# A pair's seven products in another order, with three sums formed in PSUM, and W2's gathered sums scaled by token

## The chip, the cores and the metric

The kernel runs on one core of a Trainium2 chip. The metric is the device time of one execution in microseconds (us). Five engines with queues of their own work side by side and wait for each other through semaphores: TensorE (PE, with its weight loads as PEld), VectorE (DVE), ScalarE (ACT), GpSimd (POOL) and SyncE (SP), which here only issues DMAs. Each engine takes its instructions in the order in which they stand in its queue.

## What is computed

Two layers of an encoder over 512 tokens with 1024 channels. Cut to what matters here, a layer is

```
u    = rms_norm(h)
proj = u @ w_in                      # q, k, v of three mixers, and 3 x 1024 gate logits
a, r, c = differential attention, retention, grouped-query attention
merged  = sum_n sigmoid(gate_logits[n]) * (branch[n] @ w_branch[n])
h = h + merged @ w_out
m = relu(rms_norm(h) @ w_mlp_in) ** 2          # 1024 -> 4096
h = h + m @ w_mlp_out                          # 4096 -> 1024
```

All of it is in float32 accuracy. Each matrix product is done as three passes over halves: an operand is split into `hi` (its value in TensorE's shorter float32r) and `lo` (the rest), and hi*hi + hi*lo + lo*hi is summed in PSUM.

## The kernel before

Activations lie channel-major: a tile holds 128 channels by 512 tokens. A *unit* is 128 output channels of a product, 24 matmuls over 512 tokens. Some units are done in *pairs* (the `w1` units, 16 pairs per layer, and 7 pairs of gate units per layer) with a two-by-two scheme that needs seven products instead of eight: the two units' weights form A, A12, A21, A22 and four sums S1 to S4, the tokens are cut in a left half (`lt`) and a right half (`rt`), and product n (1 to 7) is 12 matmuls over 256 tokens. `pair` (L704) runs them, `product` (L697) issues one, `right` (L686) picks its token operand, and DVE and ACT join the products into the tiles `c0` and `c1`. For W2's first three groups a scheme of the same kind works over larger blocks (`wide_product`, L1477): its seven results are added up in DRAM (`sums`) by accumulating DMAs, and `gather` (L1498) reads them back, joins them, turns them with TensorE transposes and adds them to `h`.

The weights of a unit come by one 512 KB DMA into one of two `stage` buffers. For a pair (`cut_pair`, L567) two such loads are cut: ACT casts `w_hi`, DVE subtracts `w_lo`, and DVE forms `sa` and `sb`, which are cast and cut as well. So a pair's weights become ready in the order: those of products 1 and 2 (`stage`), of products 5 and 6 (`sa`), of 3 and 7 (`sb`); those of 4 (a 512-wide `stage`) lie between.

All operations are first recorded. `Plan.order` (L347) then replays the record with a price per operation and sends each engine's queue out in the order of that replay: the operation recorded earliest goes first among those whose inputs are ready and whose buffers are free. An instruction waits on the chip for what it needs, wherever the replay put it. PSUM has pools of banks `mm` (3), `sc` (2), `tr` (2) and `av` (1); a pair takes one bank each of `mm`, `sc` and `tr`. Where a helper records an operation, the profile gives its line as L455 (matmul), L457 (transpose) or L461 (anything else).

In a layer of some 890 us the mixers with their projections come first (to about 410 us in layer 0), then the gate pairs woven with the branches' projections (`x` and `proj`, 410 to 516), the output projection (`wo`, to 560), `w1` pairs woven with W2's wide products (`x` and `wide`, 560 to 850), and W2's last group with the gather (`w` and `turn`, to 900). Layer 1 does the same some 892 us later.

Of the kernel before, what the change touches and what calls it, by code (L numbers as in the profile page):

```python
# [13 lines left out]
AF = mybir.ActivationFunctionType  # L14
ALU = mybir.AluOpType
# [456 lines left out]
class Core:  # L472
# [152 lines left out]
        self.nc.scalar.activation(out=hi, in_=src, func=AF.Copy, scale=r)  # L625
        self.nc.vector.scalar_tensor_tensor(out=lo, in0=src, scalar=r, in1=hi, op0=ALU.mult, op1=ALU.subtract)

    def passes(self, out, terms, start=True, stop=True):
        n = len(terms)
        for i, (x, y) in enumerate(terms):  # L630
            self.nc.tensor.matmul(out=out, lhsT=x, rhs=y, start=start and i == 0, stop=stop and i == n - 1)

    def transpose(self, out, in_):
        self.nc.tensor.transpose(out=out, in_=in_, identity=self.ident)
# [59 lines left out]
            return u["v"][j][p][:, lt if n == 6 else rt]  # L694
        return u["w"][j // 2][p][:, (j % 2) * 256:(j % 2) * 256 + 256]

    def product(self, out, w, u, n):  # L697
        hi, lo = w[n]
        for j in range(4):
            c = slice(j * 128, (j + 1) * 128)  # L700
            xh, xl = self.right(u, n, 0, j), self.right(u, n, 1, j)
            self.passes(out, [(hi[:, c], xh), (hi[:, c], xl), (lo[:, c], xh)], j == 0, j == 3)

    def pair(self, l, key, u, kinds, out):  # L704

        nc = self.nc
        w = self.weights(l, key)
        lt, rt = slice(0, 256), slice(256, 512)
        c0, c1 = self.g("c0"), self.g("c1")
        tmp = self.g("pu")  # L710
        x = self.psum(kinds[0], "x17")
        y = self.psum(kinds[1], "x26")
        z = self.psum(kinds[2], "x45")
        add = lambda out, p, r: nc.vector.tensor_tensor(out=out, in0=p, in1=r, op=ALU.add)
        self.product(x[:, lt], w, u, 1)
        nc.scalar.copy(out=tmp[:, lt], in_=x[:, lt])
        for j, f in enumerate(u.pop("t1", [])):
            for i in range(2):
                o = [u["u"][p][2 * j + i][:, rt] for p in range(2)]
                self.split(f[:, i * 256:(i + 1) * 256], *o)  # L720
        yield
        two = lambda v: v.rearrange("p (a b) -> p a b", a=2)
        wide = lambda v: v.unsqueeze(1).to_broadcast([128, 2, 256])
        self.product(y[:, lt], w, u, 2)
        yield
        self.product(y[:, rt], w, u, 6)
        add(two(c0), two(y), wide(tmp[:, lt]))
        yield
        self.product(z[:, rt], w, u, 5)
        yield  # L730
        self.product(x[:, rt], w, u, 7)
        add(tmp[:, rt], x[:, rt], c0[:, rt])
        add(c0[:, rt], z[:, rt], c0[:, rt])
        yield
        self.product(z[:, lt], w, u, 4)
        add(two(c1), two(z), wide(tmp[:, rt]))
        yield
        self.product(y[:, lt], w, u, 3)
        add(c0[:, rt], y[:, lt], c0[:, rt])
        out += [c0, c1]  # L740

    def add_square(self, x, acc):
# [650 lines left out]
    def mlp(self, l, mT, h, mid, load, ready):  # L1393
        nc = self.nc
        u, acc = {"u": self.new_u(), "v": [], "w": []}, None
        for i in (0, 4, 1, 5, 2, 6, 3, 7):
            p = self.psum("mm", "wo")
            hi, lo = self.weights(l, ("wo", i))
# [4 lines left out]
                self.feed_pair(h, i - 4, 2 * l + 1, u)  # L1403
            acc = self.add_square(h[i], acc)
            nc.sync.dma_start(out=mid[i], in_=h[i])
        _, _, r2 = self.rms(acc, True)
        ms = [[] for _ in range(4)]
        for what, g, i in mlp_order():
            m = ms[g]
# [18 lines left out]
                self.wide_product(l, g, i, now)  # L1428
                continue
            if i == 0:  # L1430
                gather = self.gather(h, mid, load, r2)
            if i in GATHERED:
                next(gather)
            hi, lo = self.weights(l, ("w2", g, i))
# [60 lines left out]
            else:  # L1495
                nc.gpsimd.dma_start(out=self.sums[n, s], in_=y, accum_op=ALU.add)

    def gather(self, h, mid, load, r2):  # L1498

        nc = self.nc  # L1500

        def back(n, s):
            x = self.g("wp")
            nc.sync.dma_start(out=x, in_=self.sums[n, s])
            return x

        tt = lambda out, x, y, op=ALU.add: nc.vector.tensor_tensor(out=out, in0=x, in1=y, op=op)
        u2, c = [None, None], [[None] * 4, [None] * 4]
        for s in range(2):
            p1, p2, p6, p5, p3 = (back(n, s) for n in (1, 2, 6, 5, 3))  # L1510
            tt(p2, p1, p2)
            tt(p6, p6, p1, ALU.subtract)
            tt(p5, p5, p6)
            tt(p3, p3, p5, ALU.subtract)
            c[0][s], c[0][2 + s], u2[s] = p2, p3, (p6, p5)
        for half in range(2):
            if half:
                for s in range(2):
                    p7, p4 = back(7, s), back(4, s)
                    p6, p5 = u2[s]  # L1520
                    tt(p5, p5, p7, ALU.subtract)
                    tt(p6, p6, p7, ALU.subtract)
                    tt(p6, p6, p4)
                    c[1][s], c[1][2 + s] = p6, p5
            for i in range(4):
                k = half * 4 + i
                h[k] = load(mid, k)
                p = self.psum("tr", "turn")
                for t in range(4):
                    self.transpose(p[:, t * 128:(t + 1) * 128], c[half][t][:, i * 128:(i + 1) * 128])  # L1530
                y = self.g("y")
                nc.vector.tensor_tensor(out=y, in0=p, in1=r2, op=ALU.mult)
                nc.vector.tensor_tensor(out=h[k], in0=h[k], in1=y, op=ALU.add)
            yield

    def last_unit(self, hi, lo, m, r2, x, ready):
# [163 lines left out]
```

## Time and profile before

| | |
|---|---|
| device time, 3 runs | 1787.8 us median (1786.89 to 1788.88) |
| the profiled execution | 1790.48 us, its span 1788.7 us, mean granted clock 0.996 |
| PE busy | 1751.3 us, 98% of the span |
| DVE busy | 1521.9 us, 85% |
| ACT busy | 1082.3 us, 61% |
| DMA | 201.94 MB, mean 113 GB/s |

A matmul's record is longer than the distance to the next one, since they are pipelined; the distance from start to start is what one costs on a busy PE. Names in the profile stand without buffer numbers, so the tiles `x17`, `x26` and `x45` of a pair all read `x`; products 1 to 3 and 5 are told by `u` on the right, 6 and 7 by `t23`, 4 by `t4`.

### The profile page before, as it was taken

The page shows a single profiled execution, that of the slowest core. Times are in us where ns is not written, and L with a number is a line of the kernel's source. Part 1 is how long each engine was busy: PE and PEld are TensorE (multiplying, and loading weights), DVE is VectorE, ACT ScalarE, POOL GpSimd, SP SyncE. Part 2 cuts the span into 40 slices and gives each one's busy share as a digit, 9 for nine tenths or more (in the row PEclk, how much of TensorE's full clock was granted, in tenths as well). Part 3 has the DMA queues.
Part 4 walks back from the last instruction along what each step waited for, and adds up shares of the span by engine and source line. Part 5 has one row for each costly group of instructions (what it writes and reads, how often), then busy time and mean ns, then how long its engine had stood idle before and what let it go on. Part 6 is the DMA issues. An engine that isn't in the chain of part 4 may idle for free.

```text
span 1788.7 us, 27147 instructions
## 1 busy us (share of the span) xinstructions
PE 1751.3 (98%) x10136; PEld 1529.1 (85%) x10136; DVE 1521.9 (85%) x2500; ACT 1082.3 (61%) x1864; POOL 345.5 (19%) x350
## 2 busy tenths in 40 slices
PE   8999999999999999998999999999999999999999
PEld 6887888889989999887887778888898899998887
DVE  8866797899979999898967677978999799999986
ACT  5545676784446767666445456767844467667650
POOL 2334472002210001111012334710012100011110
PEclk9999999999999999999999999999999999999999
DMA  6311212212345254746542112121133452646482
GB/s 203 106 59 55 88 55 71 60 36 95 112 166 171 95 201 99 196 95 180 192 137 68 59 62 80 49 71 59 36 95 129 149 171 99 209 99 184 95 242 88
DMA packets 76740, 201.94 MB, mean 113 GB/s; under 512 B 8896, under 2 KB 9408, under 8 KB 76608
## 3 DMA queue, kind: packets, MB, share of 16 engines
q1 hardware_dynamic: 68544, 185.53, 31.6%
q0 software_dynamic: 8064, 14.68, 5.5%
q8 instruction: 79, 1.29, 0.3%
q14 instruction: 53, 0.43, 0.1%
HBM read 169.77 MB, written 30.41 MB: 112 GB/s over the span
## 4 chain that ended last, share of the span: by engine, by line
PE 68%; DVE 15%; DMA 5%; ACT 4%; issue 4%; POOL 3%; SPq 0%; DVEq 0%; ACTq 0%; POOLq 0%
PE x L455 17%; PE wide L455 6%; PE gate L455 6%; PE proj L455 5%; PE w L455 5%; PE wo L455 5%; DVE w_lo L461 4%; DMA stage<-in_w 4%; PE c L455 4%; DVE c L461 3%; PE wtr L457 2%; PE rg L455 2%; PE gsc L455 2%; PE gav L455 2%; DVE sb L461 2%
## 5 line engine op out<-in xcount | busy, mean ns | idle before, releaser
L461 ACT CAST w_hi<-stage 128x1024 fp32r<-128x1024 f32 (+1 forms) x235 | 226.5, 968 | 214.1 <-DMA stage<-in_w 127.6
L461 DVE TENSOR_TENSOR w_lo<-stage,w_hi 128x1024 fp32r<-128x1024 f32 (+1 forms) x235 | 279.4, 1191 | 18.6 <-ACT w_hi L461 14.9
L455 PE MATMUL x<-u,w_hi 128*128 128x256 f32 x1472 | 278.8, 287 | 4.9 <-DVE c L461 4.9
L455 PEld LDWEIGHTS x<-u,w_hi 128*128 128x128 f32 x1472 | 236.5, 195 | 11.2 <-DVE c L461 7.9
L455 PE MATMUL x<-u,w_lo 128*128 128x256 f32 x736 | 210.1, 288 | 8.8 <-DVE w_lo L461 8.8
L461 POOL DMA_DIRECT2D sums<-wp x56 | 49.1, 907 | 566.8 <-ACT wp L461 558.7
L455 PEld LDWEIGHTS x<-u,w_lo 128*128 128x128 f32 x736 | 143.1, 195 | 9.9 <-DVE w_lo L461 9.7
L455 PE MATMUL wide<-w_hi,xh 128*128 128x512 f32 x336 | 129.4, 391 | 2.7 <-ACT wp L461 2.7
L455 PE MATMUL wide<-w_lo,xh 128*128 128x512 f32 x336 | 131.2, 390 | 0.0
L455 PE MATMUL wide<-w_hi,xl 128*128 128x512 f32 x336 | 130.7, 390 | 0.0
L461 ACT ACTIVATE c<-c 128x512 f32<-128x512 f32 x156 | 98.5, 632 | 51.8 <-DVE c L461 49.1
L461 DVE TENSOR_TENSOR w_lo<-A,w_hi 128x512 fp32r<-128x512 f32 x168 | 112.2, 683 | 11.3 <-ACT w_hi L461 11.2
L461 ACT CAST w_hi<-A 128x512 fp32r<-128x512 f32 x168 | 100.7, 619 | 19.2 <-DVE A L461 9.5
L455 PE MATMUL gate<-u,w_hi 128*128 128x512 f32 x320 | 106.4, 399 | 0.0
L455 PE MATMUL x<-t23h,w_lo 128*128 128x256 f32 x368 | 104.6, 284 | 0.2
L455 PE MATMUL x<-t23h,w_hi 128*128 128x256 f32 x368 | 104.3, 284 | 0.0
L455 PE MATMUL x<-t23l,w_hi 128*128 128x256 f32 x368 | 104.1, 283 | 0.0
L455 PE MATMUL c<-w_hi,u 128*128 128x512 f32 x256 | 86.1, 394 | 0.0
L461 ACT CAST w_hi<-sa 128x1024 fp32r<-128x1024 f32 x46 | 48.5, 1053 | 62.0 <-DVE sa L461 54.8
L461 POOL TENSOR_TENSOR gth<-gth,c 128x512 f32<-128x512 f32 x28 | 45.2, 1619 | 180.8 <-DVE c L461 152.8
L455 PEld LDWEIGHTS wide<-w_hi,xh 128*128 128x128 f32 x336 | 63.0, 188 | 16.2 <-ACT wp L461 4.0
L455 PEld LDWEIGHTS wide<-w_hi,xl 128*128 128x128 f32 x336 | 63.1, 188 | 12.5
(296 smaller groups left out, 5196.7 us busy)
## 6 DMA issues: line engine op xcount, KB each, us to landing
stage<-in_w SPq DMA_DIRECT2D x235, 512.0 KB, 3.6
A<-in_w SPq DMA_DIRECT2D x96, 256.0 KB, 4.5
sums<-wp POOLq DMA_DIRECT2D x56, 256.0 KB, 6.0
sums<-wp SPq DMA_DIRECT2D x28, 256.0 KB, 2.6
wp<-sums SPq DMA_DIRECT2D x28, 256.0 KB, 5.1
h<-in_x SPq DMA_DIRECT2D x16, 256.0 KB, 5.2
mid<-h SPq DMA_DIRECT2D x16, 256.0 KB, 2.0
h<-mid SPq DMA_DIRECT2D x16, 256.0 KB, 6.3
```

Of the source, the lines that this page charges most:

```text
L455: self.nc.tensor.matmul(k.pop("out"), **k)
L457: self.nc.tensor.transpose(k["out"], k["in_"], k["identity"])
L461: getattr(getattr(self.nc, o.engine), o.name)(**k)
```

## The change

Three things are done.

- `pair` runs its products in the order 1, 6, 5, 7, 2, 4, 3 instead of 1, 2, 6, 5, 7, 4, 3. Products 2, 3, 7 and 4 are added in PSUM onto what an earlier product left there: 2 onto 1 (tile `x12`), 7 onto 6 and 4 onto both (`x674`), 3 onto 5 (`x53`). Their first matmul goes without the start flag (`onto`).
- Between them ACT copies the sum as it stands out of PSUM: products 1, 6, 5, 6+7 and 1+2, five copies of 256 tokens where there was one. DVE has four additions per pair (one of 512 columns, three of 256) where it had five (two of 512, three of 256); two of the four read SBUF alone.
- `gather` no longer multiplies the turned sums in PSUM by the spread row `r2` on DVE. ACT scales the eight joined tiles by token (`rp`, a column per 128 tokens) while tokens still lie down the partitions, before the transposes, and DVE adds the turned sums to `h` straight from PSUM.

```diff
-    def product(self, out, w, u, n):
+    def product(self, out, w, u, n, fresh):
...
-            self.passes(out, [(hi[:, c], xh), (hi[:, c], xl), (lo[:, c], xh)], j == 0, j == 3)
+            self.passes(out, [(hi[:, c], xh), (hi[:, c], xl), (lo[:, c], xh)], j == 0, j == 3, not fresh)
...
-        self.product(x[:, lt], w, u, 1)
-        nc.scalar.copy(out=tmp[:, lt], in_=x[:, lt])
+        self.product(x, w, u, 1, True)
+        nc.scalar.copy(out=tmp[:, lt], in_=x)
...
+        self.product(y, w, u, 6, True)
+        nc.scalar.copy(out=c0[:, rt], in_=y)
+        yield
+        self.product(z, w, u, 5, True)
+        nc.scalar.copy(out=tmp[:, rt], in_=z)
+        yield
+        self.product(y, w, u, 7, False)
+        nc.scalar.copy(out=c0[:, lt], in_=y)
...
-        self.product(y[:, lt], w, u, 2)
+        add(two(c0), two(c0), tmp[:, lt].unsqueeze(1).to_broadcast([128, 2, 256]))
+        add(c1[:, rt], tmp[:, rt], c0[:, lt])
         yield
-        self.product(y[:, rt], w, u, 6)
-        add(two(c0), two(y), wide(tmp[:, lt]))
+        self.product(x, w, u, 2, False)
+        nc.scalar.copy(out=c0[:, lt], in_=x)
         yield
-        self.product(z[:, rt], w, u, 5)
+        self.product(y, w, u, 4, False)
+        add(c1[:, lt], y, tmp[:, lt])
         yield
-        self.product(x[:, rt], w, u, 7)
-        add(tmp[:, rt], x[:, rt], c0[:, rt])
-        add(c0[:, rt], z[:, rt], c0[:, rt])
-        yield
-        self.product(z[:, lt], w, u, 4)
-        add(two(c1), two(z), wide(tmp[:, rt]))
-        yield
-        self.product(y[:, lt], w, u, 3)
-        add(c0[:, rt], y[:, lt], c0[:, rt])
+        self.product(z, w, u, 3, False)
+        add(c0[:, rt], z, c0[:, rt])
...
+            for t, x in enumerate(c[half]):
+                nc.scalar.activation(out=x, in_=x, func=AF.Copy, scale=rp[:, t:t + 1])
...
-                y = self.g("y")
-                nc.vector.tensor_tensor(out=y, in0=p, in1=r2, op=ALU.mult)
-                nc.vector.tensor_tensor(out=h[k], in0=h[k], in1=y, op=ALU.add)
+                nc.vector.tensor_tensor(out=h[k], in0=h[k], in1=p, op=ALU.add)
```

The changed record also changes what `Plan.order` makes of it. First PE's queue in the stretch of the gate pairs, at layer 0's second gate pair. Before, product 3 (`x26` from `u`) stands inside a projection and waits for the DVE addition that empties its bank:

```order
L455 MATMUL proj_4680<-aTh_1929,w_lo_4540 128x512
L455 MATMUL proj_4680<-aTh_2309,w_hi_4523 128x512
L455 MATMUL proj_4680<-aTl_2321,w_hi_4523 128x512
L455 MATMUL proj_4680<-aTh_2309,w_lo_4540 128x512
L455 MATMUL proj_4680<-aTh_2745,w_hi_4523 128x512
L455 MATMUL x26_4608<-u04_203,w_hi_4481 128x256 [waits DVE_49]
L455 MATMUL x26_4608<-u14_220,w_hi_4481 128x256
```

In the changed kernel the same pair has product 2 (`x12` from `u`) before product 4 (`x674` from `t4`), and what product 4 waits for is ACT's copy of 6+7:

```order
L455 MATMUL x12_4619<-u06_242,w_lo_4421 128x256
L455 MATMUL x12_4619<-u07_250,w_hi_4326 128x256
L455 MATMUL x12_4619<-u17_278,w_hi_4326 128x256
L455 MATMUL x12_4619<-u07_250,w_lo_4421 128x256
L455 MATMUL x674_4566<-t4h_4126,w_hi_4388 128x256 [waits Activation_49]
L455 MATMUL x674_4566<-t4l_4142,w_hi_4388 128x256
```

The wait for DVE inside the projection has moved away; a wait for an ACT copy stands after a whole product.

Second, PE's queue at a `w1` pair of layer 0 (the one that starts at 773.4 us in the trace of before), at the first use of `sa`'s weights (product 6, `t23`). Before, products 1 and 2, both from the first load's weights, stand ahead of it:

```order
L455 MATMUL x26_8590<-u17_6046,w_hi_8425 128x256
L455 MATMUL x26_8590<-u07_6024,w_lo_8583 128x256
L455 MATMUL x26_8590<-t23h_5728,w_hi_8604 128x256 [waits Activation_49]
L455 MATMUL x26_8590<-t23l_5742,w_hi_8604 128x256
L455 MATMUL x45_8636<-u00_5719,w_hi_8604 128x256 [waits PE_49]
L455 MATMUL x45_8636<-u10_5734,w_hi_8604 128x256
L455 MATMUL x17_8587<-t23h_5728,w_hi_8625 128x256 [waits Activation_49]
L455 MATMUL x17_8587<-t23l_5742,w_hi_8625 128x256
L455 MATMUL x26_8590<-t23h_5728,w_lo_8629 128x256 [waits DVE_49]
```

Now product 1 (`x12`) alone stands ahead of it:

```order
L455 MATMUL x12_8650<-u03_6074,w_hi_8492 128x256
L455 MATMUL x12_8650<-u13_6091,w_hi_8492 128x256
L455 MATMUL x12_8650<-u03_6074,w_lo_8570 128x256
L455 MATMUL x674_8675<-t23h_5749,w_hi_8644 128x256 [waits Activation_49]
L455 MATMUL x674_8675<-t23l_5763,w_hi_8644 128x256
L455 MATMUL x53_8679<-u00_5740,w_hi_8644 128x256
L455 MATMUL x53_8679<-u10_5755,w_hi_8644 128x256
L455 MATMUL x674_8675<-t23h_5749,w_lo_8673 128x256 [waits DVE_49]
```

The first matmul on `sa`'s `w_lo` has moved from 26 places behind the pair's first on the `stage` `w_lo` to 14.

Third, ACT's queue at the next pair of the same layer (its ACT work lies at 798 to 808 us in the trace of before). Before, the copy of product 1 (`pu`) is the pair's only one:

```order
L461 COPY pu_8881<-x17_8832 128x256 [waits PE_49]
L461 CAST w_hi_8874<-A22_8155 128x512 [waits DVE_49]
L461 CAST w_hi_8916<-stage_8865 128x512 [waits DMAHW5_49]
L461 CAST w_hi_8924<-A22_8163 128x512 [waits DVE_49]
L461 CAST w_hi_8924<-A22_8170 128x512 [waits DVE_49]
L461 CAST w_hi_8955<-A12_8072 128x512 [waits DVE_49,Activation_49]
```

Now the copies of product 6, of 5 and of 6+7 (`x674`, `x53`, `x674`) stand behind the cast of a weight load that waits for its DMA:

```order
L461 COPY pu_8930<-x12_8903 128x256 [waits PE_49]
L461 CAST w_hi_8946<-stage_8895 128x512 [waits DMAHW5_49]
L461 COPY c0_8954<-x674_8922 128x256 [waits DMASW3_49,PE_49,Activation_49]
L461 CAST w_hi_8919<-A22_8205 128x512 [waits DVE_49]
L461 CAST w_hi_8965<-A22_8214 128x512 [waits DVE_49]
L461 COPY pu_8930<-x53_8942 128x256 [waits PE_49]
L461 CAST w_hi_8980<-A12_8113 128x512 [waits DVE_49]
L461 COPY c0_8954<-x674_8922 128x256 [waits PE_49]
```

Products 7 and 4 write onto the bank that the first and the last of these copies read.

## Rows read from the trace of the kernel before

**Rows 1.** The page's head and its first part: busy time, share of the span and instructions of each engine.

```profile
span 1788.7 us, 27147 instructions
PE 1751.3 (98%) x10136; PEld 1529.1 (85%) x10136; DVE 1521.9 (85%) x2500; ACT 1082.3 (61%) x1864; POOL 345.5 (19%) x350
```

**Rows 2.** Busy time by stage: the stretch, its length, then busy us and instructions of PE, PEld, DVE, ACT and POOL, TensorE's granted clock, DMA share and GB/s. Gate pairs (410 and 1302), `w1` with wide products (560 and 1452), W2's last group (850).

```profile
410.00:516.00 106.00, 103.78 (x711) 95.77 (x710) 99.13 (x130) 45.41 (x60) 20.73 (x13) 1.00 0.39 130
...
560.00:850.00 290.00, 280.80 (x1840) 258.42 (x1839) 265.83 (x473) 196.48 (x352) 24.63 (x28) 0.98 0.53 148
850.00:900.00 50.00, 50.00 (x247) 41.86 (x247) 47.08 (x71) 23.72 (x32) 0.00 (x0) 1.00 0.58 197
...
1302.00:1408.00 106.00, 103.28 (x709) 95.40 (x708) 98.72 (x129) 45.51 (x59) 20.76 (x13) 1.00 0.40 131
1452.00:1740.00 288.00, 283.09 (x1873) 260.64 (x1872) 269.64 (x481) 199.60 (x357) 24.49 (x28) 0.99 0.55 154
```

**Rows 3.** Two pieces of the chain that ended last, in order of time: start, length, engine and tile, matmuls.

```profile
500.53 8.63 PE x L455 x72
...
516.09 43.59 PE wo L455 x192
```

**Rows 4.** Waits in the stretch 380 to 520 us: who waited for whom, us in total, times, longest.

```profile
PEld x L455 <- DVE c L461: 3.9, 5, 1.0
PE x L455 <- DVE c L461: 2.2, 4, 0.6
```

**Rows 5.** The same of 1290 to 1410 us.

```profile
PEld x L455 <- DVE c L461: 4.4, 5, 1.5
...
PE x L455 <- DVE c L461: 2.7, 4, 1.1
```

**Rows 6.** PE's instructions in order of time around the first and the last of the eight waits for `c` in the two stretches of gate pairs: start, length, instruction, and in brackets the idle time before it and what ended it.

```profile
427.87 0.39 PE L455 MATMUL proj<-aTh,w_hi 128*128 128x512 f32 x1
428.71 0.51 PE L455 MATMUL x<-u,w_hi 128*128 128x256 f32 x2 [0.45 <-DVE c L461]
...
1383.50 0.40 PE L455 MATMUL proj<-cTl,w_hi 128*128 128x512 f32 x1
1384.49 0.50 PE L455 MATMUL x<-u,w_hi 128*128 128x256 f32 x2 [0.59 <-DVE c L461]
```

**Rows 7.** Groups of DVE and ACT instructions by form: count, busy us, mean ns of one, idle time before them and its releasers.

```profile
L461 DVE TENSOR_TENSOR c<-x,pu 128x512 f32<-128x512 f32 x92 | 62.9, 684 | 8.0 <-PE x L455 6.6 <-ACT pu L461 0.4
L461 DVE TENSOR_TENSOR c<-x,c 128x256 f32<-128x256 f32 x92 | 38.5, 419 | 3.0 <-PE x L455 1.2
...
L461 DVE TENSOR_TENSOR y<-turn,rs 128x512 f32<-128x512 f32 x16 | 10.5, 683 | 1.2 <-PE turn L457 1.1
...
L461 ACT ACTIVATE gE<-gE,grc 128x512 f32<-128x512 f32 x64 | 45.4, 725 | 6.1 <-DVE grc L461 5.7 <-DVE gcol L461 0.4
...
L461 ACT COPY pu<-x 128x256 f32<-128x256 f32 x46 | 17.1, 372 | 7.8 <-PE x L455 7.2 <-ACT w_hi L461 0.4
```

**Rows 8.** Waits in the stretch 560 to 850 us.

```profile
ACT w_hi L461 <- DMA stage<-in_w: 28.7, 13, 4.9
...
PE x L455 <- DVE w_lo L461: 5.3, 2, 3.2
```

**Rows 9.** DVE's instructions in order of time at the cut of the weights of the `w1` pair that starts at 773.4 us.

```profile
772.47 1.21 DVE L461 TENSOR_TENSOR w_lo<-stage,w_hi 128x1024 fp32r<-128x1024 f32 x1
...
776.02 1.21 DVE L461 TENSOR_TENSOR w_lo<-sa,w_hi 128x1024 fp32r<-128x1024 f32 x1
```

**Rows 10.** PE's instructions in order of time at the last `w1` pair of layer 0.

```profile
834.75 0.52 PE L455 MATMUL x<-u,w_hi 128*128 128x256 f32 x3
838.45 0.58 PE L455 MATMUL x<-u,w_lo 128*128 128x256 f32 x1 [3.18 <-DVE w_lo L461]
...
844.30 0.28 PE L455 MATMUL x<-t23h,w_lo 128*128 128x256 f32 x1
```

**Rows 11.** DVE's at the same pair.

```profile
837.17 1.22 DVE L461 TENSOR_TENSOR w_lo<-stage,w_hi 128x1024 fp32r<-128x1024 f32 x1
...
841.05 1.22 DVE L461 TENSOR_TENSOR w_lo<-sa,w_hi 128x1024 fp32r<-128x1024 f32 x1
```

**Rows 12.** PE's at the last `w1` pair of layer 1.

```profile
1724.42 0.39 PE L455 MATMUL x<-u,w_lo 128*128 128x256 f32 x1 [3.46 <-DVE w_lo L461]
...
1729.24 0.28 PE L455 MATMUL x<-t23h,w_lo 128*128 128x256 f32 x1
```

**Rows 13.** DVE's at that pair.

```profile
1727.02 1.22 DVE L461 TENSOR_TENSOR w_lo<-sa,w_hi 128x1024 fp32r<-128x1024 f32 x1
```

**Rows 14.** ACT's instructions in order of time at 798 to 805 us.

```profile
798.40 0.38 ACT L461 COPY pu<-x 128x256 f32<-128x256 f32 x1
...
804.53 0.62 ACT L461 CAST w_hi<-stage 128x512 fp32r<-128x512 f32 x1 [4.89 <-DMA stage<-in_w]
```

**Rows 15.** PE's in the same time.

```profile
800.37 0.40 PE L455 MATMUL x<-u,w_hi 128*128 128x256 f32 x2
...
802.77 0.28 PE L455 MATMUL x<-t23h,w_lo 128*128 128x256 f32 x1
```

**Rows 16.** One stretch with the columns of rows 2.

```profile
840.00:860.00 20.00, 20.00 (x131) 18.78 (x131) 18.23 (x29) 14.04 (x20) 0.00 (x0) 0.90 0.73 260
```

More of the change, by code (lines that the diff above doesn't have):

```diff
@@ L626, in split_scaled, with passes @@
         self.nc.vector.scalar_tensor_tensor(out=lo, in0=src, scalar=r, in1=hi, op0=ALU.mult, op1=ALU.subtract)
-    def passes(self, out, terms, start=True, stop=True):
+    def passes(self, out, terms, start=True, stop=True, onto=False):
         n = len(terms)
+        more = {"skip_group_check": True} if onto else {}
         for i, (x, y) in enumerate(terms):
-            self.nc.tensor.matmul(out=out, lhsT=x, rhs=y, start=start and i == 0, stop=stop and i == n - 1)
+            self.nc.tensor.matmul(out=out, lhsT=x, rhs=y, start=start and i == 0 and not onto,
+                                  stop=stop and i == n - 1, **more)
     def transpose(self, out, in_):
@@ L710, in pair @@
         tmp = self.g("pu")
[L711 to L714, printed above, removed]
-        self.product(x[:, lt], w, u, 1)
-        nc.scalar.copy(out=tmp[:, lt], in_=x[:, lt])
+        x = self.psum(kinds[0], "x12")[:, lt]
+        y = self.psum(kinds[1], "x674")[:, lt]
+        z = self.psum(kinds[2], "x53")[:, lt]
+        add = lambda o, p, r: nc.vector.tensor_tensor(out=o, in0=p, in1=r, op=ALU.add)
+        self.product(x, w, u, 1, True)
+        nc.scalar.copy(out=tmp[:, lt], in_=x)
         for j, f in enumerate(u.pop("t1", [])):
@@ L721, in pair @@
         yield
+        self.product(y, w, u, 6, True)
[6 more added lines that the diff above has]
+        nc.scalar.copy(out=c0[:, lt], in_=y)
         two = lambda v: v.rearrange("p (a b) -> p a b", a=2)
-        wide = lambda v: v.unsqueeze(1).to_broadcast([128, 2, 256])
-        self.product(y[:, lt], w, u, 2)
+        add(two(c0), two(c0), tmp[:, lt].unsqueeze(1).to_broadcast([128, 2, 256]))
+        add(c1[:, rt], tmp[:, rt], c0[:, lt])
         yield
-        self.product(y[:, rt], w, u, 6)
-        add(two(c0), two(y), wide(tmp[:, lt]))
+        self.product(x, w, u, 2, False)
+        nc.scalar.copy(out=c0[:, lt], in_=x)
         yield
-        self.product(z[:, rt], w, u, 5)
+        self.product(y, w, u, 4, False)
+        add(c1[:, lt], y, tmp[:, lt])
         yield
-        self.product(x[:, rt], w, u, 7)
-        add(tmp[:, rt], x[:, rt], c0[:, rt])
-        add(c0[:, rt], z[:, rt], c0[:, rt])
-        yield
-        self.product(z[:, lt], w, u, 4)
-        add(two(c1), two(z), wide(tmp[:, rt]))
-        yield
-        self.product(y[:, lt], w, u, 3)
-        add(c0[:, rt], y[:, lt], c0[:, rt])
+        self.product(z, w, u, 3, False)
+        add(c0[:, rt], z, c0[:, rt])
         out += [c0, c1]
@@ L1405, in mlp @@
             nc.sync.dma_start(out=mid[i], in_=h[i])
-        _, _, r2 = self.rms(acc, True)
+        _, rp, r2 = self.rms(acc, True)
         ms = [[] for _ in range(4)]
@@ L1430, in mlp @@
             if i == 0:
-                gather = self.gather(h, mid, load, r2)
+                gather = self.gather(h, mid, load, rp)
             if i in GATHERED:
@@ L1496, in wide_product, with gather @@
                 nc.gpsimd.dma_start(out=self.sums[n, s], in_=y, accum_op=ALU.add)
-    def gather(self, h, mid, load, r2):
+    def gather(self, h, mid, load, rp):
         nc = self.nc
```

## The prediction

> **What bounds the kernel now.** I read the page's first part, then the busy time by stage, then PE's waits in the stages that the change touches, and last the instructions in order of time at the longest waits. PE is busy in 98% of the span [rows 1], and that is close to its own pace: 72 matmuls of a pair take 8.63 us, 0.120 us from start to start, and 192 matmuls of 512 columns take 43.59 us, 0.227 each [rows 3]. The change takes no matmul away, so all that it can save is time in which PE waits. The reader should look in the stages for how much of that there is: PE's busy time falls short of the stretch by 2.2 and 2.7 us in the two stretches of gate pairs, and by 9.2 and 4.9 us in the two of `w1` pairs [rows 2]; in W2's last group it is nothing [rows 2]. A record is longer than a slot, so a wait shows shorter than it is: 427.87 to 428.71 is 0.84 us for a slot of 0.23, a loss of 0.61 where the idle time says 0.45 [rows 6]. By these rows 19 us in all can be won back there, by the starts somewhat more; the rest of the 1788.7 does not hang on this change.
>
> **Gate pairs.** All that PE waits for there is DVE's `c`: 2.2 us in four waits in layer 0 and 2.7 us in four in layer 1 [rows 4, 5], counted on the weight loads 3.9 and 4.4. It is product 3, which writes into the bank that holds products 2 and 6 until DVE, busy 94% of this stretch [rows 2], has added them up. In the new order no product waits for DVE's additions inside a pair: 7 and 4 wait for ACT's copies, each with another product in between. From start to start the first of the eight waits costs 0.61 us and the last 0.99 - 0.23 = 0.76 [rows 6]; with a mean of 0.7 to 0.8 that is 8 x 0.75 = 6.0 us. The bounds are 2.2 + 2.7 = 4.9 and 3.9 + 4.4 = 8.3 [rows 4, 5]. I take 6.0, by the starts. The new waits I cost at nothing: a copy of 256 columns takes 0.372 us [rows 7], the product in between 12 x 0.12 = 1.44 us, and ACT is busy only 45.4 of 106 us here [rows 2], with 7 x 4 = 28 copies or 10.4 us to come. If ACT should stand behind a cast as a gating copy comes, each costs up to what the cast is late.
>
> **Work moved between engines.** Of the `c<-x,pu` additions (684 ns, 92) one per pair goes; the 256-wide ones stay three per pair [rows 7]: 46 x 0.684 = 31.5 us less on DVE. The gather's multiplications take 16 x 0.683 = 10.9 us more off it [rows 7]. ACT gets 4 x 46 copies of 0.372, 68.4 us, and 16 scalings, which with a scale per partition are nearest to `gE` at 0.725: 11.6 us [rows 7]. In 560 to 850 us DVE falls from 266 by 16 x 0.684 = 11 us, and ACT rises from 196 to about 225 of 290 [rows 2]. The gather's own part lies in a stage without PE idle time [rows 2], beside W2's matmuls: nothing either way. The scaling puts an ACT step between DVE's joining and the transposes; I bound it at 0 to 4 x 0.725 = 2.9 us per layer, if no other W2 matmul covers it, and take 0, since 8 x 24 of them stand ready.
>
> **`w1` pairs.** Here PE waits for weights. The longest waits are of one make: a load lands late, ACT's cast waits for it (28.7 us in 13 waits), DVE's `w_lo` follows and PE waits (5.3 us in two waits) [rows 8]. The new order of products speaks against the change here. `w_lo` of `stage` ends at 773.68 and that of `sa` at 777.23 [rows 9], 3.55 us later. Before, 26 matmuls or 3.1 us lay between their first uses; now 14, or 1.7 us. So a pair whose weights come just in time loses 3.55 - 1.7 = 1.9 us where it lost 0.4.
>
> Such losses do not add up, though, since the weights come by DMA and DVE, not by PE: a PE that has waited once finds the next weights earlier. What counts is the last pair. In layer 0 its first `w_lo` matmul starts at 838.45 after 3.2 us of waiting, and its first on `sa`'s `w_lo` at 844.30 [rows 10], although that was ready at 841.05 + 1.22 = 842.27 [rows 11]. In between stand 27 matmuls of which each takes 0.21 us: the granted clock in 840 to 860 is 0.90 [rows 16], a mean of a piece at 1.2 GHz and the rest at 2.4. In the new order 14 matmuls stand in between, and the 11 others that had waited for DVE's additions are done before the wait: 14 x 0.21 = 2.9 us bring PE to 841.4, it waits for 842.3, and so is where it was at 844.30 by 842.3, 2.0 us earlier. In layer 1 it is 1727.02 + 1.22 = 1728.24 against 1729.24 [rows 12, 13], 1.0 us. Together 3.0 us, if the weights come when they came. If PE still ran these at half the clock for as long as before, it is nothing: bounds 0 and 3.0 plus what DVE, with less to do, brings the weights forward. That is at most one addition of 0.684 less for each of the eight pairs in the second half, 5.5 us per layer, and at least nothing, or a loss of as much as ACT's copies (3 x 0.372 per pair) delay the casts. I take 0.5 us per layer, near the lower end, since at these places DVE itself waits for the DMA.
>
> The Trainium skill (TensorE: Matmul & The Clock Gate, Part 1) has PE's clock fall to half after an idle stretch and says that there is no step in between. The trace agrees: matmuls at 0.21 us after the wait of 3.2 us [rows 10], where 0.12 is the busy pace. By this rule alone each new wait of that length would cost another 2 us or so of slow matmuls.
>
> **The sum.** 6.0 + 3.0 + 1.0 = 10.0 us less than the profiled execution's 1790.5, so 1780.5. The median of the three runs is 1787.8, 2.7 us under that execution; against it I forecast 1777.8.
>
> **Rivals.** *ScalarE's queue, slower than before.* The copies stand behind casts that wait for a DMA. At 799 us ACT stood 4.89 us before such a cast [rows 14], while PE ran products 6, 5 and 7 (product 7 ends with the matmul at 802.77) [rows 15]. In the new queue the copy of product 6 stands behind that cast: it would end at 804.53 + 0.62 + 0.37 = 805.5, where product 7 could have begun at 800.4 [rows 15], a wait of 5 us. With 13 such waits of 2.2 us on average [rows 8], about half in reach of a gating copy, that is 6 x 2 = 12 us per layer. The same reasoning as above speaks against it: where the weights are late anyway, a wait for the copy takes the place of one for weights. It decides if the weights then slide with PE, because `w` buffers and wide products free later. With half of it, 12 us on both layers, less the gates' 6: 1794; in full 1806.
>
> The Trainium skill (PSUM — Partial Sum Buffer, Engine vs sequencer instructions) calls ScalarE's queue a strict first-in first-out, which speaks for this rival; the trace agrees as far as nothing ran on ACT in these 4.89 us [rows 14].
>
> *The gates' gain, and no more.* The earlier demand for `sa`'s weights and the copies take back what the last pair gives, and some of the 6 us: 1785 to 1790. For it: DVE is busy 266 of 290 us in 560 to 850 [rows 2], so a late `w_lo` is not sped up by much. Against it: what is lost early is absorbed.
>
> *DVE was what made the weights late.* With 11 us less of it per layer the loads are asked for earlier, and the waits of 3.2 and 3.5 us [rows 10, 12] shrink by half and more: another 5 to 8 us, 1771.
>
> **How the numbers follow.** Forecast, 1773 to 1784: 0.50. DVE's relief in full, below 1773: 0.11. The gates' gain eaten, 1784 to 1791.4: 0.21. ScalarE's queue, above that: 0.18. This kernel's runs can tell a difference of about 0.2%, 3.6 us. Faster by more than that: 0.50 + 0.11 + a little of the third for its lower edge, 0.61; within it 0.21; slower 0.18. The range that leaves out a tenth on each side is 1769 to 1795.
>
> **What would show it.** In the gate stretches PE's waits for DVE `c` are gone and its busy time fills the 106 us to within 0.5. At the `w1` pairs from 690 us on, PE waits for `w_lo` at `t23` instead of at `u`, 1 to 2 us each, and for ACT's copies behind late casts; yet the last pair's product 6 starts its `w_lo` at about 842 - 3 = 839 us in layer 0 and 1728 - 9 = 1719 in layer 1, the 3 and 9 us being what was won before them. `wo` and W2's last group take as long as before. I am wrong if waits of PE for ACT stand in the gate stretches, if the last `sa` weights of a layer are ready more than 2 us later than now by the layer's own clock, or if W2's last group shows PE waiting for the scaled tiles.

## The result, and the profile after

The changed kernel takes 1774.7 us against 1787.9 us (medians of four executions each): a ratio of 0.9926, 95% interval 0.9903 to 0.9948, or 13 us faster with 9 to 17 as the interval. One of the changed kernel's four executions took 1891.0 us at a granted clock of 0.85; the other three took 1772.2 to 1775.4, with 1774.0 in the middle. Run again beside the later experiments it had 0.9924 (0.9905 to 0.9944). The profiled execution took 1772.2 us.

The head of the page after, which answers to [rows 1]:

```profile
span 1770.4 us, 27228 instructions
PE 1744.6 (99%) x10136; PEld 1525.3 (86%) x10136; DVE 1484.3 (84%) x2438; ACT 1139.0 (64%) x2064; POOL 339.9 (19%) x350
```

Busy time by stage after, with the columns of [rows 2] (the same stages: `wo` begins 2.3 us earlier in layer 0 and 17.0 in layer 1; the `w1` stretches are as long as before, so where the stage has become shorter they hold some of W2's last group, in which PE is full):

```profile
408.00:514.00 106.00, 105.90 (x729) 98.69 (x729) 96.29 (x126) 55.96 (x91) 19.12 (x13) 1.00 0.41 135
558.00:848.00 290.00, 288.33 (x1909) 265.19 (x1908) 268.93 (x477) 221.93 (x432) 24.61 (x28) 1.00 0.57 161
848.00:898.00 50.00, 50.00 (x236) 41.59 (x235) 40.48 (x56) 22.09 (x30) 1.23 (x2) 1.00 0.52 158
1285.00:1391.00 106.00, 105.76 (x730) 98.67 (x729) 96.73 (x125) 55.87 (x90) 19.66 (x14) 1.00 0.41 134
1435.00:1723.00 288.00, 283.44 (x1879) 260.34 (x1879) 263.60 (x467) 217.35 (x423) 24.46 (x28) 1.00 0.56 156
```

Both gate stretches are full to within 0.3 us, where 2.2 and 2.7 were missing [rows 2]. The `w1` stretch of layer 0 lacks 1.7 us where it lacked 9.2; that of layer 1 lacks 4.6 where it lacked 4.9, so the two layers did not gain alike. DVE fell by 1521.9 - 1484.3 = 37.6 us and ACT rose by 56.7 (less than the 80 that the added instructions last, since the records of neighbours in a queue overlap by up to 0.1 us each).

Whom PE waited for, first from 558 to 848 us, then from 1435 to 1723 us (engine, line and tile; whom; us in total, times, longest):

```profile
PE x L455 <- ACT c L461: 1.4, 3, 0.9
```

```profile
PE x L455 <- ACT c L461: 4.2, 5, 1.1
PE x L455 <- DVE w_lo L461: 0.2, 1, 0.2
```

The long waits for weights [rows 8, 10, 12] are gone. In their place stand short ones for ACT's copies, all at product 7 or 4. With the long waits went the half clock: after, every stage above reads 1.00.

PE's waits are shorter in these lists than they are from start to start, so for what follows I summed, over all matmuls and transposes, the time to the next start less the slot (0.120 us for 256 columns, 0.228 for 512, 0.113 for a transpose). Slow matmuls at half the clock count in it too. All of PE's 51.4 us of such loss fell to 33.1, and 51.4 - 33.1 = 18.3 is the difference of the two spans, 1788.7 and 1770.4. By stage it was 3.3 and 3.8 us in the gates and 15.3 and 8.2 in the `w1` stages; it is 0.7, 0.7, 3.1 and 6.9. The mixers, `wo` and W2's last group are unchanged to within 0.7 us each.

### The profile page after: what moved, and what is told of

Its sections match the earlier page's. It is cut to its first block, busy times and chain, and to the rows that moved or that the text cites. A ratio compares the mean times of both kernels' runs of the same rounds, so it can differ in the third digit from the quotient of the medians.

```text
span 1770.4 us, 27228 instructions
## 1 busy us (share of the span) xinstructions
PE 1744.6 (99%) x10136; PEld 1525.3 (86%) x10136; DVE 1484.3 (84%) x2438; ACT 1139.0 (64%) x2064; POOL 339.9 (19%) x350
## 4 chain that ended last, share of the span: by engine, by line
PE 73%; DVE 11%; DMA 6%; ACT 5%; issue 3%; POOL 2%; SPq 0%; ACTq 0%; DVEq 0%; POOLq 0%
PE x L455 19%; PE wide L455 7%; PE proj L455 6%; PE gate L455 6%; DMA stage<-in_w 6%; PE w L455 5%; PE wo L455 5%; PE c L455 4%; DVE w_lo L461 4%; PE wtr L457 2%; PE rg L455 2%; PE gsc L455 2%; PE gav L455 2%; PE dsc L455 2%; PE rq L455 1%
## 5 line engine op out<-in xcount | busy, mean ns | idle before, releaser
L461 ACT ACTIVATE c<-c 128x512 f32<-128x512 f32 x156 | 94.0, 628 | 19.0 <-DVE c L461 17.3
L455 PEld LDWEIGHTS x<-t23h,w_hi 128*128 128x128 f32 x368 | 70.3, 191 | 5.9 <-ACT c L461 5.3
L461 POOL TENSOR_TENSOR gth<-gth,c 128x512 f32<-128x512 f32 x28 | 40.8, 1465 | 178.1 <-DVE c L461 178.0
L455 PEld LDWEIGHTS wide<-w_hi,xl 128*128 128x128 f32 x336 | 63.1, 188 | 13.1
L455 PEld LDWEIGHTS wide<-w_lo,xh 128*128 128x128 f32 x336 | 63.1, 188 | 12.5
```

The lines of the kernel that those rows point to most:

```text
L455: self.nc.tensor.matmul(k.pop("out"), **k)
L461: getattr(getattr(self.nc, o.engine), o.name)(**k)
```

## The experiments

All ratios are to the kernel before on the same chip, with their 95% interval. The losses are those of one profiled execution: both gate stretches together, then both `w1` stages together.

| run | ratio | gates | `w1` |
|---|---|---|---|
| before | 1 | 7.1 | 23.4 |
| after | 0.9926 (0.9903 to 0.9948) | 1.4 | 10.0 |
| gather alone | 0.9993 (0.9979 to 1.0008) | 7.2 | 18.0 |
| gate pairs alone | 0.9964 (0.9949 to 0.9980) | 1.8 | 17.6 |
| `w1` pairs alone | 0.9955 (0.9941 to 0.9969) | 7.2 | 13.1 |
| after, DVE work put back | 0.9992 (0.9977 to 1.0007) | 1.7 | 21.2 |
| before, two additions less | 0.9916 (0.9896 to 0.9936) | 1.0 | 8.3 |
| after, product 2 early | 0.9960 (0.9946 to 0.9973) | 0.4 | 13.6 |
| after, three copies more | 0.9947 (0.9928 to 0.9965) | 2.3 | 9.2 |
| after, addition on GpSimd | 1.0019 (1.0006 to 1.0033) | 0.9 | 21.1 |
| after, order 1, 6, 5, 2, 7, 3, 4 | 0.9941 (0.9920 to 0.9962) | 0.3 | 12.8 |
| after, one addition less | 0.9934 (0.9916 to 0.9951) | 1.7 | 12.2 |
| after, again | 0.9924 (0.9905 to 0.9944) | 1.5 | 11.7 |
| after, planner's hop 250 | 0.9915 (0.9897 to 0.9933) | 0.0 | 10.2 |

**The parts one by one.** The first kernel has the new `gather` with the old `pair`; the second and third choose the pair by stage:

```diff
+    def pair(self, l, key, u, kinds, out):
+        return (self.pair_new if key[0] == "gate" else self.pair_old)(l, key, u, kinds, out)
```

> The gather's scaling on ScalarE, the pairs as before. My sum had this part at nothing: 1787.9 us, within 3 us. If DVE's load is what sets the time, 10.9 us less of it in W2's last group would show there, but PE had no idle time in that group, so this theory expects no more than 2 us as well. If the planner's order by itself moves the time (every change of one instruction reorders all queues behind it), it can be 5 us off either way, with the waits at the last w1 pair of layer 0 (3.3 us, at 835 us before) grown or gone, although nothing there is changed.

> The new pair for the gates alone, w1 pairs and the gather as before. By my sum 6.0 us faster: 1782; PE's waits for DVE's c gone between 410 and 516 us and between 1302 and 1408 us, the long waits for weights at 746, 835 and 1721 us (2.3, 3.3 and 3.6 us) still there, some 3 us earlier or 6. If the waits in the w1 stage are an accident of the planner's order, they change here too, and the time is 1775 or 1788 rather than 1782.

> The new pair for w1 alone, gates and gather as before. From the two traces: 51.4 - 33.1 = 18.3 us less waiting of PE, of it 5.8 in the gates, so 12.5 here if the parts add up: 1775 to 1776. By my sum 4 us: 1784. If the gain in the w1 stage needed the loads to come earlier through the gates, it is below 4 us, and the waits of 3 us at the last pair of each layer are still there.

The gather alone gives -1.3 us (-3.8 to +1.4): no difference that can be told. The gates give -6.4 (-9.1 to -3.6), the `w1` pairs -8.0 (-10.5 to -5.5); with the gather's -1.3 that is -15.7 where the whole change has -13.2, within the intervals. So the parts add up.

Three kernels with the old `w1` pairs lost 23.4, 18.0 and 17.6 us in these stages, in mean 19.7, and four with the new ones 10.0, 13.1, 11.7 and 10.2, in mean 11.2. The difference, 8.4, is what the third run measured; the 23.4 - 10.0 = 13.4 of the first two traces was an execution of before with much waiting beside one of after with little. (The 13.1 is from the slowest of that run's twelve executions.) By layer, the same means fall by 7.3 us in layer 0 and by 1.2 in layer 1, so layer 0 has most of the gain in these executions too. Why, no run shows.

**DVE's load, put back and taken away.** In the changed kernel one more addition of 512 columns per pair; in the kernel before two of 256 left out:

```diff
         add(c1[:, rt], tmp[:, rt], c0[:, lt])
+        add(self.g("junk"), c0, c0)
```

```diff
-        add(tmp[:, rt], x[:, rt], c0[:, rt])
-        add(c0[:, rt], z[:, rt], c0[:, rt])
...
-        add(two(c1), two(z), wide(tmp[:, rt]))
+        add(two(c1), two(z), wide(tmp[:, lt]))
```

> The changed kernel, with one more addition of 512 columns on DVE per pair (0.68 us, read by nobody), so that DVE has as much to do per pair as before. If DVE's load is what made the weights late, the w1 stage of layer 0 loses its 12 us again and the time is 1784 to 1787. If it is the order (no product waits for DVE's sums, so none is put off and the weight buffers come free on time), it stays within 3 us of the changed kernel's 1774.7. Between these, both have a part.

> The kernel before, with two of its five additions per pair left out (256 columns each, 0.42 us: the sums with products 7 and 5 are not formed, so the outputs lack them). DVE has 0.84 us less per pair, a little more than the change takes, with the products, the banks and ScalarE as before. If DVE's load is what made the weights late, the w1 stages gain 12 us or more, 1773 to 1777; the gates keep their waits for c (6 us between them), or a part of them. If it takes the new order of products and banks, it stays at 1784 to 1788. The second way in which it could go: the waits for c shrink too, since the addition that product 3 waits for comes sooner; then 1770.

The second is the clear one. With the old products, the old order and ScalarE's old load, 46 x 0.84 = 38.5 us less of DVE bring 15.0 us (11.4 to 18.5), as much as the whole change. Less of DVE is therefore enough by itself for a gain of this size, and for the gates too: with a shorter queue product 3's sums come in time, and 1.0 us of waiting is left there of 7.1. What is taken away is more than busy time, since DVE also stood idle up to 8.8 us before these two groups of additions (5.8 before `pu<-x,c`, 3.0 before `c<-x,c`), mostly for PE's products.

The first lost 11.8 us against the changed kernel, as that theory asks, but its trace shows that it does not test it alone. Waits from 560 to 850 us:

```profile
ACT c L461 <- DVE junk L461: 6.8, 7, 2.0
...
PE x L455 <- ACT c L461: 3.5, 4, 1.8
```

The added instruction reads `c0`, and ACT's copy of product 2 goes into `c0`, so ACT stood 6.8 us behind the very addition I put in, and PE behind ACT. How much of the 11.8 is DVE's load and how much this wait stays open. That the gates kept their gain (1.7) does say that there the new order, too, is enough by itself. And by the lists PE does not wait for `w_lo` once in the `w1` stages of this run, while with two additions less such waits remain, 3.0 us in layer 0 and 1.1 in layer 1. That speaks for the order, and not DVE's relief, as what ended the waits for `w_lo`; here waits for ACT took their place.

**How DVE makes a load late.** The prediction read the landing of the last pair's weights as the DMA's lateness. The issue shows that this is half of it. DVE and then SP in the kernel before:

```profile
825.16 0.69 DVE L461 TENSOR_TENSOR w_lo<-stage,w_hi 128x512 fp32r<-128x512 f32 x1
825.76 0.68 DVE L461 TENSOR_TENSOR sb<-stage,sa 128x512 f32<-128x512 f32 x1
```

```profile
825.88 0.97 SPq L461 DMA_DIRECT2D stage<-in_w  x2
```

The same place after:

```profile
814.39 0.68 DVE L461 TENSOR_TENSOR w_lo<-stage,w_hi 128x512 fp32r<-128x512 f32 x1
814.99 0.68 DVE L461 TENSOR_TENSOR sb<-stage,sa 128x512 f32<-128x512 f32 x1
```

```profile
815.10 0.97 SPq L461 DMA_DIRECT2D stage<-in_w  x2
```

In both, the first load goes out within 0.03 us of the end of the previous pair's `w_lo<-stage` (825.85, 815.07), and the `x2` row holds the second, some 0.6 us on, as `sb` ends: the two `stage` buffers are free only when DVE has cut the pair before. So a late DVE shows one pair later as a late DMA. The loads go out 10.8 us earlier, and PE's turn at the pair's first `w_lo` comes 8.3 us earlier (826.77, first row below; before, without the wait, it was at 834.75 + 3 x 0.12 = 835.11 [rows 10]), so the weights have gained on PE. PE and DVE at the last pair of layer 0, after:

```profile
826.77 0.28 PE L455 MATMUL x<-u,w_lo 128*128 128x256 f32 x1
...
828.93 0.40 PE L455 MATMUL x<-u,w_hi 128*128 128x256 f32 x2
829.45 0.39 PE L455 MATMUL x<-t23h,w_lo 128*128 128x256 f32 x1
```

```profile
828.17 1.22 DVE L461 TENSOR_TENSOR w_lo<-sa,w_hi 128x1024 fp32r<-128x1024 f32 x1
```

`sa`'s weights are ready at 829.39 and used at 829.45. By the starts PE's turn was at 828.93 + 2 x 0.12 = 829.17, a loss of 0.28 us.

The other half is the transfer, which was slow too. DVE's first instruction on the last pair's weights, which waits for the second load, in the kernel before, in the changed one, and in the old one with two additions less:

```profile
835.96 0.69 DVE L461 TENSOR_TENSOR sa<-stage 128x512 f32<-128x512 f32 x1 [4.23 <-DMA stage<-in_w]
```

```profile
823.41 0.69 DVE L461 TENSOR_TENSOR sa<-stage 128x512 f32<-128x512 f32 x1 [2.46 <-DMA stage<-in_w]
```

```profile
826.63 0.69 DVE L461 TENSOR_TENSOR sa<-stage 128x512 f32<-128x512 f32 x1 [4.24 <-DMA stage<-in_w]
```

The second load went out at 826.51, 815.74 and 817.17, and so took 9.4, 7.7 and 9.4 us. The page before has 3.6 us as the median of all these loads:

```profile
stage<-in_w SPq DMA_DIRECT2D x235, 512.0 KB, 3.6
```

With two additions less the load goes out 9.3 us earlier than before, but PE is there 9.1 us earlier as well (825.97), the transfer takes as long, and PE still waits 2.99 us at this pair where it waited 3.18. So less of DVE alone did not end the wait on which the prediction had built. From the second load's issue to PE's turn there were 8.6 us before, 8.8 with two additions less and 11.0 after. What made this longer and the transfer shorter in the changed kernel, no run shows. There the late load is still felt, through ACT: the cast of the first load waits for it, the copy that product 7 needs stands behind the cast, and PE waits for the copy (ACT, then PE):

```profile
821.11 1.05 ACT L461 CAST w_hi<-stage 128x1024 fp32r<-128x1024 f32 x1 [2.75 <-DMA stage<-in_w]
```

```profile
822.48 0.39 PE L455 MATMUL x<-t23h,w_hi 128*128 128x256 f32 x1 [0.94 <-ACT c L461]
```

**The order of the products, and ScalarE's copies.** Product 2 early, in a half bank of its own, and added to product 1 by DVE; the last addition is left out and the copy of product 2 goes where nobody reads it, so that both engines have as many instructions as after. Then three copies more that nobody reads:

```diff
+        self.product(x[:, rt], w, u, 2, True)
+        yield
         self.product(y, w, u, 6, True)
...
-        self.product(x, w, u, 2, False)
-        nc.scalar.copy(out=c0[:, lt], in_=x)
+        add(c0[:, lt], x[:, rt], tmp[:, lt])
+        nc.scalar.copy(out=self.g("junk")[:, lt], in_=x[:, rt])
...
-        add(c0[:, rt], z, c0[:, rt])
```

> The changed kernel with product 2 in second place again, in a half of its own (order 1, 2, 6, 5, 7, 4, 3), so that sa's weights are wanted after 24 products' matmuls and not after 12. Product 2 is added to product 1 by DVE (256 columns), ScalarE copies it into a buffer that nobody reads, and the last addition, of product 3, is left out (the output lacks products 5 and 3 there): DVE and ScalarE have as many instructions of the same sizes as in the changed kernel. By the run with the added DVE work the new pair loses about 5 us in the w1 stages when DVE's work is equal to before's; if that is the earlier demand for sa's weights, this kernel is 3 to 6 us faster than the changed one, 1769 to 1772. If the earlier demand costs nothing, 1773 to 1776.

> The changed kernel with three more copies of 256 columns per pair on ScalarE (0.372 us each, of products 6, 5 and 7, into a buffer that nobody reads). If ScalarE's queue is what costs the w1 stages their remaining waits, 16 pairs x 1.1 us more work per layer make them worse by as much as the copies of the change did: 5 us or more, 1780 and up. If ScalarE has room (76% busy in 560 to 850 us), 1774 to 1777.

Both expectations of a cost failed. Wanting `sa`'s weights later made the kernel not faster but some 6 us slower than after (0.9960 to 0.9926), although the two intervals just meet; in its trace 2 of the 6 us stand in layer 1's first mixer (a wait of 2.0 us for ACT's `rkh`) and most of the rest in the `w1` stages, in waits for ACT. And 46 x 3 x 0.372 = 51 us more of ScalarE cost about 4 us (0.9947 to 0.9924 or 0.9926), which the intervals do not tell from nothing, and none of it in the `w1` stages (9.2). ScalarE's load as such is not what is left.

**What is left.** Five more runs: the changed kernel with the 512-column addition of the `w1` pairs on GpSimd (its edit stands below), with two products between 6 and 7, with one addition less, as it is, and with `HOP = 250.0`, the planner's price for the way from one engine to another:

```diff
+        engine = nc.gpsimd if key[0] == "w1" else nc.vector
+        engine.tensor_tensor(out=two(c0), in0=two(c0), in1=tmp[:, lt].unsqueeze(1).to_broadcast([128, 2, 256]), op=ALU.add)
-        add(two(c0), two(c0), tmp[:, lt].unsqueeze(1).to_broadcast([128, 2, 256]))
```

> The changed kernel with the 512-column addition of each w1 pair on GpSimd, where additions of this size take 1.3 to 1.5 us; DVE has another 0.68 us less in each of the 32 w1 pairs. If DVE's load still sets the remaining waits of the w1 stages (3.1 and 6.9 us), up to half of them goes: 1769 to 1772. If ScalarE's copies set them, nothing: 1773 to 1776; and if the copy of product 2, which waits until the sums have been read, now stands before other ScalarE work for GpSimd, or GpSimd's own transfers of the wide products come late, it is slower: 1777 to 1782.

> The changed kernel with the products in the order 1, 6, 5, 2, 7, 3, 4: between product 6 and product 7, which is added onto it, stand two products (2.9 us) and not one, and ScalarE's copy of products 1 and 2 stands behind that of product 7. The waits of PE for ScalarE's copies, about 1 us each, are the longest that are left in the w1 stages (4.2 us in five waits at product 7 or 4 in layer 1). If they are what is left to win, this is 3 to 6 us faster than the changed kernel run beside it. If DVE's and the DMA's weights come next, right behind, it is within 2 us of it.

> The changed kernel with the 512-column addition of each pair left out (product 1 is missing in two of the sums): another 0.68 us less of DVE per pair, 31.5 us in all, as much as the change took. If DVE's load still sets the waits, a part of the last 10 us in the w1 stages goes: 1767 to 1771 where the changed kernel beside it has 1774. If it is used up, within 2 us of the changed kernel: what is left is ScalarE's and the mixers'.

> The changed kernel once more, on the same chip as the others of this call, so that they are compared with it and not with its runs elsewhere: 0.990 to 0.995 of the kernel before, 1770 to 1775, by every theory.

> The changed kernel with one number of the planner changed: 250 instead of 200 ns for the way from one engine to another, which alters no work and puts the queues in another order. If such an order by itself moves the time by 5 us or more, the gains of single parts of that size could be chance; if it stays within 3 us of the changed kernel beside it, they are not. The DVE theory says nothing on it but that DVE's busy time stays.

31.5 us less of DVE once more leave the time at 1774.7 beside 1772.8. So DVE's relief is used up, as far as this run shows it: its queues are in another order, and PE waits in it for ACT's `pu`, 3.5 and 3.0 us in the two `w1` stages, which the changed kernel does not. The other order of the queues gives 1771.1, so this one change of the planner's order moves the whole by 2 us, not by the size of the parts measured above.

A wider gap between products 6 and 7 brought nothing, and the reason stands in ACT's queue of that kernel, with PE beneath it:

```profile
819.91 0.37 ACT L461 COPY pu<-x 128x256 f32<-128x256 f32 x1
824.44 1.04 ACT L461 CAST w_hi<-stage 128x1024 fp32r<-128x1024 f32 x1 [4.16 <-DMA stage<-in_w]
825.39 0.36 ACT L461 COPY c<-x 128x256 f32<-128x256 f32 x1
```

```profile
825.81 0.39 PE L455 MATMUL x<-t23h,w_hi 128*128 128x256 f32 x1 [2.20 <-ACT c L461]
```

ACT stood 4.16 us before a cast whose load had not landed, with the copy that product 7 needs behind it. The changed kernel has the same at its longest wait; ACT, then PE:

```profile
1650.87 0.37 ACT L461 COPY c<-x 128x256 f32<-128x256 f32 x1 [0.71 <-PE x L455]
1653.74 0.62 ACT L461 CAST w_hi<-stage 128x512 fp32r<-128x512 f32 x1 [2.50 <-DMA stage<-in_w]
...
1655.57 0.37 ACT L461 COPY c<-x 128x256 f32<-128x256 f32 x1
```

```profile
1656.00 0.39 PE L455 MATMUL x<-t4h,w_hi 128*128 128x256 f32 x1 [1.09 <-ACT c L461]
```

No gap of one or two products covers that. What would, a cast that stands behind the copies or weights that land before their cast's turn, was not tried. None of the runs that compute the whole beat the changed kernel by more than its interval.

## Why the prediction was right, and where its sizes were off

The forecast was 1777.8 with a range of 1769 to 1795; measured were 1774.7 and, again, 1772.8. The 10.0 us of the sum lie inside the measured 9 to 17.

**Gate pairs, 6.0 us: right.** 5.7 by the starts, 6.4 by the run with them alone. The new waits for ACT, taken at nothing, are none in layer 0 and 0.2 us in layer 1. What the prediction left out is that the shorter DVE queue alone would have done it.

**Work moved: right to the instruction.** The `c<-x,pu` additions fell as counted, and ACT's groups after are these (count, busy us, mean ns, idle before them):

```profile
L461 ACT COPY c<-x 128x256 f32<-128x256 f32 x138 | 51.1, 372 | 29.2 <-PE x L455 19.8 <-DVE c L461 8.5
...
L461 ACT COPY pu<-x 128x256 f32<-128x256 f32 x92 | 34.0, 372 | 13.6 <-PE x L455 11.8 <-ACT wp L461 1.4
...
L461 ACT ACTIVATE wp<-wp,rs 128x512 f32<-128x512 f32 x16 | 11.2, 724 | 0.2
```

Of 230 copies 184 are new, and the scalings took 0.724 us each where 0.725 was taken from `gE`. The gather's part at nothing is what its own run shows, and W2's last group stays full at 50.00 of 50 us.

**`w1` pairs, 4.0 us: the mechanism half right, the size half of what came.** The run with them alone has 8.0. Three terms did not come as reckoned.
- "I take 0.5 us per layer, near the lower end, since at these places DVE itself waits for the DMA." The bound was 5.5 per layer. Two additions less in the old kernel cut the `w1` losses from a mean of 19.7 to 8.3 us (4.0 of the 11.4 are matmuls at half the clock, of which that execution has none). At layer 0's last pair the reason given holds, for PE still waits there. What it passed over are the other waits of the stage: by the lists PE waited 9.1 us in layer 0 (5.3 for `w_lo`, 2.0 for `c`, 1.8 for ACT's `wp`) and 4.8 in layer 1, and with two additions less 5.0 and 1.7.
- The cost of needing `sa`'s weights after 14 matmuls. By the lists PE waits for `w_lo` in the changed kernel once, 0.2 us; the forecast waits of 1 to 2 us at `t23` are not there, and needing them later gained nothing.
- The 3.0 us of the two last pairs, "if the weights come when they came". They did not: product 6 started on `w_lo` at 829.5 and 1710.2, not at 839 and 1719. Counted from the start of `wo`, that is 844.30 - 829.45 - 2.3 = 12.5 us earlier in layer 0, where the sum had 2.0, and 1729.24 - 1710.17 - 17.0 = 2.1 in layer 1, where it had 1.0. These hold all that was won in the stage up to there, so no run shows the term by itself.

That the whole came within 5 us of the forecast therefore owes something to luck: the gates' term was right, but 3.0 of the 4.0 beside it rested on weights coming at their old times, which they did not.

In the two profiled executions the matmuls at half the clock went with the long waits, and the sum had no term for them. Three stretches of the kernel before, in the columns of [rows 2]:

```profile
743.00:757.00 14.00, 11.87 (x87) 11.66 (x86) 10.91 (x17) 7.74 (x13) 0.00 (x0) 0.88 0.63 188
834.00:848.00 14.00, 10.82 (x69) 10.62 (x68) 11.01 (x16) 7.36 (x10) 0.00 (x0) 0.76 0.66 231
1720.00:1732.00 12.00, 8.54 (x59) 8.34 (x58) 10.06 (x15) 5.62 (x7) 0.00 (x0) 0.86 0.67 227
```

The granted clock is 0.88, 0.76 and 0.86. As a mean of the two levels, 1.2 and 2.4 GHz, these are 3.4, 6.7 and 3.4 us at the lower one, and half of each is lost: 1.7 + 3.4 + 1.7 = 6.8 us in that execution. Others had less: 1.7 with the gather alone and 3.4 with the gates alone. Nor are the new `w1` pairs free of it: of their four executions two had none, the one with the `w1` pairs alone 1.7 and the one with the other hop 3.4, after waits for ACT of 2.0 to 2.8 us (the granted clock is 0.79 over 8 us at each of these places). So of the 8.4 us between the means, 4.0 - 1.3 = 2.7 are the clock's.

**The rivals.** *ScalarE's queue* was seen rightly and priced too high: PE waits for copies behind casts that wait for a load, as in the rows above, but for 1.4 and 4.2 us by the lists (4.2 and 3.8 in the second profile), not 12 per layer. As the prediction argued against it, such a wait takes the place of one for weights. The Trainium skill (PSUM — Partial Sum Buffer, Engine vs sequencer instructions) holds that this queue is strictly in order; the 2.50 and 4.16 us in which nothing behind the cast ran agree. *The gates' gain and no more* falls with the run of the `w1` pairs alone. *DVE was what made the weights late*, given 0.11, named the engine rightly: relief of DVE alone brings as much as the change. But the waits of 3.2 and 3.5 us, which it had shrink by half and more, are 2.99 and 1.1 in that run, so in layer 0 it is not by this wait that the relief pays. Its price of 5 to 8 us on top of the forecast was too much, since 8.4 in the `w1` stages is 4.4 more than the forecast had.

What stays open is how the `w1` gain divides between DVE's relief and the new order of products and banks. Either run that might tell has a second change in it: the addition put back made ACT wait, and the early product 2 changed ACT's waits as well. What the traces do show, one execution of each, is that relief alone left layer 0's last wait for `w_lo` where it was, and that the new order had no such wait even with DVE's old work.

## What to carry to other kernels

When a load lands late, look at what released its buffer as well as at the transfer: here an engine that was busy 85% of the span set its start, by the buffers that it was late to empty, while the transfer itself took 7.7 to 9.4 us where 3.6 is the median. And starting it earlier helps only if the one that waits does not come earlier by as much. Before pricing a change from one trace, compare the waits of the same stage in several executions: three kernels with the same pair in it lost 17.6 to 23.4 us there. And a dummy instruction that is to cost an engine only time must not read a buffer that another engine is about to write.

## What the runs showed of the hardware

**GpSimd and DVE stand in each other's way.** With 32 additions on GpSimd the time rose by 3.4 us over before and by some 17 over after. DVE lost 32 instructions, worth 21.9 us, but is as busy as after (1483.0 and 1484.3 us). How much of the 17 us comes from that is not shown, since DVE also waited 11.9 us for GpSimd's sums, and ACT's copies for DVE behind it. GpSimd, then DVE, from 576 us in that kernel:

```profile
576.31 1.48 POOL L461 TENSOR_TENSOR c<-c,pu 128x512 f32<-128x512 f32 x1 [7.81 <-ACT c L461]
```

```profile
575.96 0.68 DVE L461 TENSOR_TENSOR sa<-stage 128x512 f32<-128x512 f32 x1
576.56 1.78 DVE L461 TENSOR_TENSOR sb<-stage 128x512 f32<-128x512 f32 x1
```

The DVE instruction that began second took 1.78 us where its like take 0.68, and ended 0.55 us after GpSimd's. Twenty microseconds later it is the other way; GpSimd's begins while a DVE addition is running:

```profile
596.55 3.37 POOL L461 TENSOR_TENSOR c<-c,pu 128x512 f32<-128x512 f32 x1 [8.57 <-ACT c L461]
```

```profile
596.28 0.41 DVE L461 TENSOR_TENSOR c<-c,c 128x256 f32<-128x256 f32 x1
596.62 1.21 DVE L461 TENSOR_TENSOR w_lo<-stage,w_hi 128x1024 fp32r<-128x1024 f32 x1
597.75 0.41 DVE L461 TENSOR_TENSOR xl<-c,xh 128x256 fp32r<-128x256 f32 x1
598.09 0.68 DVE L461 TENSOR_TENSOR w_lo<-A,w_hi 128x512 fp32r<-128x512 f32 x1
```

Here four DVE instructions in a row run at their usual length and GpSimd's takes 3.37. The Trainium skill (SBUF — State Buffer, Who interferes with whom) has the two engines share a pair of ports under an exclusive lock, and a DVE instruction with two SBUF inputs contend with a GpSimd instruction that reads SBUF. Both pairs of rows agree, as far as one engine runs on at its usual length and the other is held up: all these DVE instructions read two SBUF tiles.

**Not every long wait costs the clock.** In the kernel before, waits of 2.1, 3.2 and 3.5 us were each followed by matmuls at the lower clock. Two others were not: with the gather alone PE waited 2.50 us at 748 us, and with two additions left out 2.99 us at 826, and the granted clock of those stretches is 1.00 (first the one, then the other; PE's row and the stretch, columns of [rows 2]):

```profile
750.48 0.39 PE L455 MATMUL x<-u,w_lo 128*128 128x256 f32 x1 [2.50 <-DVE w_lo L461]
```

```profile
745.00:757.00 12.00, 9.50 (x79) 9.29 (x79) 9.01 (x14) 5.84 (x10) 0.00 (x0) 1.00 0.57 158
```

```profile
829.12 0.39 PE L455 MATMUL x<-u,w_lo 128*128 128x256 f32 x1 [2.99 <-DVE w_lo L461]
```

```profile
824.00:840.00 16.00, 12.90 (x105) 12.49 (x104) 13.37 (x19) 9.49 (x13) 0.00 (x0) 1.00 0.77 256
```

So the slow matmuls behind such a wait, 1.7 us and once 3.4, are a cost that some executions pay and others do not, a part of why the same stage takes different times.
